# Output projection of the second layer as seven products of quarters per two token tiles, with the gate folded into weight forms made during the attention

## The chip, the cores and the metric

The kernel runs on one core of one Trainium2 chip. The core has a matrix engine (PE, TensorE), a vector engine (DVE, VectorE), an activation engine (ACT, ScalarE), a general engine (POOL, GpSimd) and a queue engine for transfers (SP, SyncE). They run side by side, each through its own instructions in order, and wait for one another by semaphores. The metric is the device time of one execution in microseconds, lower is better; the time before is the median of three runs.

## The reference, cut to what matters

Two layers work on 1024 latent tokens of width 1024, with 256 context tokens in front. The first layer mixes by windowed attention, the second by latent attention (16 heads, 64 wide). Only the end of the second layer is touched:

```python
ox = lax.map(lambda qq: attend(qq[0], qq[1], kn_all, kr_all, v_all), ...)   # softmax attention
ox = jnp.moveaxis(ox, 0, 1).reshape(b, T, B_WIDTH)
yx = (ox * jax.nn.silu(gx)) @ w_out          # (1024 x 1024) @ (1024 x 1024): the output projection
...
x = x + gate_x[:, None] * yx                 # gate_x: one factor per output column
...
return rms_norm(x, final_g)                  # x / sqrt(mean(x*x) + eps) * final_g, per token
```

All matrix products keep nearly full float precision: each operand is cut into a high part (rounded to the format that TensorE takes) and a low part (the rest), and a product is three matmuls, high x high, low x high, high x low (`mm3`, lines 283 to 287).

## The kernel before

The program builds one long list of instructions. From line 1081 on the order of the instructions on every engine is the order in which the program writes them. A planner (class Plan) reorders a stretch before the attention of the second layer and ends at line 1987; the units and the output stage that follow are not planned.

**The units.** The attention of the second layer runs in 16 units (class UnitB): 8 pairs of heads times two halves of 512 tokens. In the loop of line 2003 unit `ui` goes through ten steps c, one per 128 keys. A step holds, in written order: six score matmuls (`score`, line 1813) for the 512 queries of both heads; `top` of the next unit (line 1779, four or eight matmuls into two banks of PSUM), followed by two VectorE maxima over these banks (lines 1785 and 1787); in step 0, the gate multiplications of an earlier unit on GpSimd (`gate`, line 1858) and their store to `og_d` (line 1860); the other four score matmuls; and one exponential on ScalarE from PSUM (line 1823) into a ring of nine buffers, added by GpSimd into a running sum (lines 1827 and 1829; in the last unit by VectorE). The banks of `top` come from a ring of three (`topb`, banks 0, 1, 2), two per step. Scores use banks 3 to 6, in pairs, and bank 7 takes the product with the values (`PV`, line 1836). Behind the ten steps come PV, the sums by a column of ones (`fin2`, line 1847), the maxima turned into the next unit's shift (line 1797), two reciprocals (`inv`, line 1853), and for some units keys (`make_K`) or values (`make_V`) of later ones.

**The weights.** `wo_pieces` (line 1872) is a generator. Each call loads one piece of b_w_out (128 x 512) and splits an earlier one into `WoB`: a ScalarE copy makes the high part (line 280), a GpSimd subtraction the low part (line 281). It is called in step 2 of units 1 to 11, in step 7 of unit 6, and in steps 2 and 7 of units 12 and 13, 16 pieces in all.

**The output stage.** `out_tiles` (line 1916) goes over 8 tiles of 128 tokens. For each, `fetch_out` has loaded the gated attention (`og_d`) and x, `cut_out` has split it, and two halves of 512 columns take 8 x 3 matmuls each, over 8 chunks of 128 channels. From PSUM VectorE multiplies by the gate `gx1` (line 1948) and adds x (line 1949), ScalarE sums squares (line 1950), GpSimd makes the reciprocal root (lines 1960 to 1962), and VectorE scales by it and by final_g (line 1972) ahead of the store. The last 256 columns of the last tile use weights with the gate folded in (`fold_gate`, lines 1911 to 1914, GpSimd) and take x by two matmuls against an identity.

Transfers named `load` are issued by SP, in written order; one that has to wait holds up those behind it.

## Time and profile before

| | us |
|---|---|
| median of 3 runs | 1486.98 (1486.8 to 1489.12) |
| the profiled execution, its time | 1486.25 |
| its span in the profile | 1484.2 |
| TensorE busy | 1463.4 |
| VectorE busy | 1063.3 |
| ScalarE busy | 736.9 |
| GpSimd busy | 804.4 |

The granted TensorE clock was 0.999 of full speed. In the rows that follow, a row of the time line gives the start in us from the span's start, the busy time in us, the engine, the line of the kernel, the operation, what is written and read, how often (x4: four such instructions merged into one row), and in brackets how long the engine had been idle and what released it. A row of a line's view gives the count, the shortest, median and longest time in ns, the first and last start, and the shapes. PEld is the load of weights into TensorE, which overlaps its matmuls.

### The profile page before, as it was taken

To read this page: it belongs to the slowest core of one execution; us is meant where nothing else is said; L and a number is where in the kernel's file an instruction comes from. 1 tells how busy PE (TensorE), PEld (TensorE's weight loads), DVE (VectorE), ACT (ScalarE), POOL (GpSimd) and SP (SyncE) were. 2 spreads that over 40 slices of the span, in tenths; PEclk is the share of its full clock that TensorE was granted. 3 is DMA by queue.
4 is the path that set the end of the run, shared out by engine and by line. 5 is a ranking of instruction groups with operands and counts; after the bars stand their busy time and mean duration, and the time that the engine had idled before them with its cause. 6 is when DMAs were issued, how large, how long until landed. Compare 5 with 4: busy or idle time off the path is not lost.

```text
span 1484.2 us, 25103 instructions
## 1 busy us (share of the span) xinstructions
PE 1463.4 (99%) x9050; PEld 1184.9 (80%) x9050; DVE 1063.3 (72%) x2031; ACT 736.9 (50%) x1405; POOL 804.4 (54%) x736
## 2 busy tenths in 40 slices
PE   7999999999999999999999999999999999999998
PEld 4888888888888888889888888767777767866687
DVE  4787789738778888877988777666576566566764
ACT  4421222359888878877554432443454344444321
POOL 2463366356454444456300240798788788789371
PEclk9999999999999999999999999999999999999999
DMA  9555644573343333338344566011122211120442
GB/s 336 171 171 172 212 153 166 192 240 113 120 141 121 101 100 100 100 99 261 99 116 121 173 237 200 16 46 48 53 61 68 60 47 61 54 68 28 154 149 86
DMA packets 146964, 186.01 MB, mean 125 GB/s; under 512 B 12812, under 2 KB 100492, under 8 KB 146840
## 3 DMA queue, kind: packets, MB, share of 16 engines
q1 hardware_dynamic: 141864, 177.75, 38.0%
q10 hardware_dynamic: 4976, 6.66, 1.3%
q8 instruction: 71, 1.16, 0.3%
q14 instruction: 53, 0.43, 0.1%
HBM read 134.02 MB, written 46.15 MB: 121 GB/s over the span
## 4 chain that ended last, share of the span: by engine, by line
PE 91%; DVE 4%; issue 2%; DMA 1%; ACT 1%; POOL 1%; SPq 0%; ACTq 0%; POOLq 0%; DVEq 0%
PE PB L285 15%; PE PB L286 14%; PE PB L287 14%; PE PB L1813 13%; PE PB L1836 9%; PE PB L737 5%; PE PB L1779 5%; PE PB L727 5%; PE PB L697 3%; PE PB L698 3%; PE PB L911 1%; PE PB L1847 1%; DVE arena_r L281 1%; PE PB L916 1%; PE PB L756 1%
## 5 line engine op out<-in xcount | busy, mean ns | idle before, releaser
L285 PE MATMUL PB<-arena_r 128*128 128x512 f32 (+2 forms) x1200 | 439.4, 366 | 1.1 <-DVE arena_f L1261 1.1
L286 PE MATMUL PB<-arena_r 128*128 128x512 f32 (+2 forms) x1200 | 433.7, 361 | 0.1
L287 PE MATMUL PB<-arena_r 128*128 128x512 f32 (+2 forms) x1200 | 433.3, 361 | 0.0
L1829 POOL TENSOR_TENSOR arena_f<-arena_f 128x1024 f32<-128x1024 f32 x120 | 285.7, 2381 | 8.2
L285 PEld LDWEIGHTS PB<-arena_r 128*128 128x128 f32 x1200 | 226.3, 189 | 45.7 <-issue 9.0
L287 PEld LDWEIGHTS PB<-arena_r 128*128 128x128 f32 x1200 | 226.3, 189 | 33.4
L286 PEld LDWEIGHTS PB<-arena_r 128*128 128x128 f32 x1200 | 226.4, 189 | 32.1 <-POOL arena_r L281 0.6
L1813 PE MATMUL PB<-arena_r 64*128 64x512 f32 (+1 forms) x1600 | 225.9, 395 | 0.0
L1823 ACT ACTIVATE arena_f<-PB 128x1024 f32<-128x1024 f32 x160 | 164.3, 1027 | 112.1 <-PE PB L1813 83.8
L1785 DVE TENSOR_REDUCE krF<-PB 128x1 f32<-128x512 f32 (+1 forms) x264 | 166.9, 677 | 66.2 <-PE PB L1779 66.2
L1813 PEld LDWEIGHTS PB<-arena_r 64*128 64x128 f32 (+1 forms) x1600 | 173.7, 185 | 17.2 <-issue 5.2
L704 DVE CUSTOM_DVE_ANT_0 arena_f<-PB,arena_f,small 128x256 f32<-128x256 f32 (+1 forms) x288 | 148.2, 525 | 51.6 <-PE PB L698 33.3
L280 ACT CAST arena_r<-PB 128x512 fp32r<-128x512 f32 (+2 forms) x207 | 115.2, 563 | 113.9 <-PE PB L287 73.3
L281 DVE TENSOR_TENSOR arena_r<-PB,arena_r 128x512 fp32r<-128x512 f32 (+2 forms) x207 | 134.2, 660 | 36.4 <-ACT arena_r L280 36.0
L1836 PE MATMUL PB<-arena_f 128*64 128x512 f32 x640 | 145.9, 595 | 0.0
L281 POOL TENSOR_TENSOR arena_r<-arena_f,arena_r 128x512 fp32r<-128x512 f32 (+1 forms) x64 | 88.2, 1393 | 103.9 <-ACT arena_r L280 92.9
L280 ACT CAST arena_r<-arena_f 128x512 fp32r<-128x512 f32 (+1 forms) x142 | 82.2, 610 | 90.1 <-PE PB L287 29.5
L710 ACT ACTIVATE arena_f<-arena_f,small 128x640 f32<-128x640 f32 (+2 forms) x160 | 119.1, 744 | 15.5 <-DVE small L704 13.9
L507 DVE SCALAR_TENSOR_TENSOR arena_f<-arena_f,small 128x512 f32<-128x512 f32 x98 | 114.0, 1208 | 9.7 <-DMA arena_f<-ada_w 9.4
L737 PE MATMUL PB<-arena_r 128*128 128x512 f32 x336 | 118.6, 429 | 0.0
L1779 PE MATMUL PB<-arena_r 64*128 64x512 f32 (+1 forms) x768 | 110.6, 355 | 0.1
L727 PE MATMUL PB<-ident,arena_f 128*128 128x128 f32 x672 | 108.7, 272 | 0.1
(219 smaller groups left out, 2079.1 us busy)
## 6 DMA issues: line engine op xcount, KB each, us to landing
arena_f<-ada_w SPq DMA_DIRECT2D x96, 256.0 KB, 3.9
arena_r<-q_d SPq DMA_DIRECT2D x160, 128.0 KB, 2.8
arena_f<-a_w_in SPq DMA_DIRECT2D x40, 256.0 KB, 3.5
arena_f<-b_w_in SPq DMA_DIRECT2D x36, 256.0 KB, 3.2
arena_f<-x SPq DMA_DIRECT2D x16, 512.0 KB, 6.0
q_d<-arena_f SPq DMA_DIRECT2D x16, 512.0 KB, 3.0
arena_r<-qn_d SPq DMA_DIRECT2D x16, 512.0 KB, 5.1
g_d<-arena_f ACTq DMA_DIRECT2D x20, 256.0 KB, 3.9
```

The costliest lines, as they stand in the source:

```text
L280: nc.scalar.copy(hi, src)
L281: (lo_eng or nc.vector).tensor_sub(lo, src, hi.bitcast(F32))
L285: nc.tensor.matmul(o, ah, bh, start=first, stop=False)
L286: nc.tensor.matmul(o, al, bh, start=False, stop=False)
L287: nc.tensor.matmul(o, ah, bl, start=False, stop=last)
L727: nc.tensor.transpose(pt[:, h, :], self.Ps[h][:, ci * 128 : ci * 128 + 128], ident)
L737: nc.tensor.matmul(self.pv, V[:, self.chunks[ci], self.g, :], PT[:, s], start=ci == 0 and s == 0, stop=ci == self.m - 1 and s == 1,)
L1779: nc.tensor.matmul(bank[:, o : o + n], self.q[r, s, bs], k[r, 0, n0 : n0 + n], start=s == 0, stop=s == 2)
L1785: nc.vector.reduce_max(self.mxp[:, e, b : b + 1, i], bank[:, 0:n], AX.X)
L1813: nc.tensor.matmul(PB[:, b + e, :], k[r, s, cs], q[r, sq], start=i == 0, stop=i == 4)
L1829: eng.tensor_add(acc, acc, E)
L1836: nc.tensor.matmul(PB[r, 7, :], Vq[:, c, h, :], E[:, e], start=c == 0, stop=c == NT - 1)
```

## The change

Two tiles of 128 tokens (rows a1, a2, each in two halves of 512 channels: a11, a12, a21, a22) times the weight in four quarters of 512 x 512 (B11, B12, B21, B22) is made from seven products of 128 x 512 by 512 x 512 instead of eight. With the gate folded in (each column times its gate factor), the weight forms are B11, B21, B22, T1 = B12 - B11, T2 = B22 - T1, T3 = B22 - B12 and T4 = T2 - B21. The left sides are a11, a12, a22, s1 = a21 + a22, s2 = s1 - a11, s3 = a11 - a21 and s4 = a12 - s2. The order of the products is a11 B11, a12 B21, s2 T2, s3 T3, s1 T1, s4 B22, a22 T4, and sums of their results give the four quarters of the output. There are four such sets.

The weight forms are made by a new `wo_pieces`, one small piece of work per call, called in steps 1 to 6 of every unit from unit 2 on until it is used up: a multiplication by the gate, a difference, or a cut (ScalarE copy, then a VectorE subtraction). 18 of the 28 cuts go by one buffer, `wtmp`, to DRAM (`wb_d`) and are loaded back later (`wo_back`): ten for k = 2, 3 in units 13 and 14, T3 in the last unit and behind it, T4 in the first set of the output stage. The left sides are made by `all_cuts`, three of them behind the last steps of the last unit, two behind it, one more with each product. `out_sets` replaces `out_tiles`; the last unit's `fin2`, `inv` and `gate` move into its first set, behind the first, second and third product.

```diff
-    WoB = [r_at(o, 2, 1024) for o in (56, 64, 72, 96, 104, 48, 80, 88)]
+    homes = {
+        "B11": (56, 76, 80, 118), "B22": (60, 96, 84, 122), "T1": (64, 100, 88, 126), "T2": (68, 104, 92, 130),
+        "B21": (72, 108, 114, 134), "T3": (0, 4, 8, 12), "T4": (16, 20, 24, 28),
+    }
+    WB = {n: [r_at(o, 2, 512) for o in at] for n, at in homes.items()}
+    away = [(n, k) for n in homes for k in range(4) if k > 1 or n in ("T3", "T4")]
+    away = {at: wb_d[i] for i, at in enumerate(away)}
...
+    gx1 = r_at(48, 1024).bitcast(F32)
+    wtmp = r_at(52, 2, 512)
+    def wo_cut(n, k, src):
+        dst = wtmp if (n, k) in away else WB[n][k]
+        split(dst[:, 0], dst[:, 1], src)
+        if (n, k) in away:
+            load(out=away[n, k], in_=wtmp.bitcast(F32))
+    def wo_back(n, k):
+        load(out=WB[n][k].bitcast(F32), in_=away[n, k])
     def wo_pieces():
...
+        g1, g2 = gx1[:, 0:512], gx1[:, 512:1024]
+        def fetch(dst, i, j, k):
+            load(out=dst, in_=t["b_w_out"][i * 512 + k * 128 : i * 512 + k * 128 + 128, j * 512 : j * 512 + 512])
+        def fetch_abc(k, what):
+            for dst, i, j in what:
+                if k < 4:
+                    fetch(dst, i, j, k)
+        V = nc.vector
+        load(out=gx1, in_=gate_d[1, 0, :].partition_broadcast(128))
+        fetch_abc(0, ((a, 0, 0), (b, 0, 1), (c, 1, 1)))
+        yield
+        for k in range(4):
+            V.tensor_mul(a, a, g1)
+            yield
+            wo_cut("B11", k, a)
+            yield
+            V.tensor_mul(b, b, g2)
+            yield
+            V.tensor_sub(a, b, a)
+            yield
+            wo_cut("T1", k, a)
+            yield
+            V.tensor_mul(c, c, g2)
+            yield
+            wo_cut("B22", k, c)
+            yield
+            V.tensor_sub(b, c, b)
+            yield
+            wo_cut("T3", k, b)
+            fetch(b, 1, 0, k)
+            yield
+            V.tensor_sub(c, c, a)
+            yield
+            wo_cut("T2", k, c)
+            fetch_abc(k + 1, ((a, 0, 0),))
+            yield
+            V.tensor_mul(b, b, g1)
+            yield
+            wo_cut("B21", k, b)
+            yield
+            V.tensor_sub(b, c, b)
+            yield
+            wo_cut("T4", k, b)
+            fetch_abc(k + 1, ((b, 0, 1), (c, 1, 1)))
+            yield
...
+    rawr = [[r_at(o, 8, 128) for o in at] for at in ((138, 142), (48, 52))]
+    xr1 = Ring(F, [52, 56, 38, 48], 1024)
+    yr = Ring(F, [22, 26, 30, 34], 1024)
+    sr1 = Ring(F, [4, 6, 8, 44, 46], 512)
+    ur = Ring(F, [10, 12, 14, 16, 18, 20], 512)
+    cuts = [[r_at(o, 4, 128), r_at(l, 4, 128)] for o, l in ((146, 148), (112, 150), (32, 34), (36, 38), (40, 42), (44, 46))]
+    pso1 = Banks(0, 1, 2, 3, 4, 6)
+    WAY = ("B11", "B21", "T2", "T3", "T1", "B22", "T4")
+    cut_n = [0]
+    def cut(src, eng):
+        hi, lo = cuts[cut_n[0] % 6]
+        cut_n[0] += 1
+        split(hi, lo, src if len(src.shape) == 3 else shp(src, 4, 128), eng)
+        return hi, lo
+    def cut_set(n):
+        (a11, a12), (a21, a22) = ([x.bitcast(F32)[:, 4 * h : 4 * h + 4] for h in range(2)] for x in rawr[n % 2])
+        P = nc.gpsimd
+        eng = P if n == 0 else nc.vector
+        s1, s2, s3, s4 = (shp(sr1.next(), 4, 128) for _ in range(4))
+        yield cut(a11, eng)
+        yield cut(a12, eng)
+        P.tensor_add(s1, a21, a22)
+        P.tensor_sub(s2, s1, a11)
+        yield cut(s2, eng)
+        P.tensor_sub(s3, a11, a21)
+        yield cut(s3, nc.vector)
+        yield cut(s1, nc.vector)
+        P.tensor_sub(s4, a12, s2)
+        yield cut(s4, nc.vector)
+        yield cut(a22, P)
+    def all_cuts():
+        for n in range(4):
+            yield from cut_set(n)
+    def out_product(A, name, cs=slice(0, 512)):
+        ps = pso1()[:, cs]
+        for k in range(4):
+            mm3(ps, [A[s][:, k] for s in range(2)], [WB[name][k][:, s, cs] for s in range(2)], k == 0, k == 3)
+        return ps
...
+        for n in range(4):
+            xa, xb = xs
+            ya, yb = yr.next(), yr.next()
+            sa, sb = sm_ring(), sm_ring()
+            last = n == 3
+            for j in range(7):
+                if not (last and j == 6):
+                    ps = out_product(A.pop(0), WAY[j])
+                x = next(made, None)
+                if x:
+                    A.append(x)
+                while late:
+                    late.pop(0)()
+                if j == 0:
+                    p1 = ur.next()
+                    nc.scalar.copy(p1, ps)
+                    if n:
+                        tile_out(2 * n - 1, *prev)
+                if j == 1:
+                    V.tensor_add(ya[:, lo], ps, p1)
+                    quad(ya, xa, lo, sa, 0)
+                if j == 5 and n < 2:
+                    fetch_raw(n + 2)
+                if n == 0 and j == 0:
+                    u.fin2(psd)
+                if n == 0 and j in (1, 2):
+                    u.inv(j - 1)
+                    u.gate(256 * j - 256, 256 * j)
+                if n == 0 and j == 2:
+                    for k in range(4):
+                        wo_back("T4", k)
+                if j == 2:
+                    u2 = ur.next()
+                    V.tensor_add(u2, ps, p1)
+                if j == 3:
+                    u3 = ur.next()
+                    V.tensor_add(u3, ps, u2)
+                if j == 4:
+                    u4 = ur.next()
+                    V.tensor_add(u4, ps, u2)
+                    V.tensor_add(yb[:, up], ps, u3)
+                    quad(yb, xb, up, sb, 1)
+                    if n < 3:
+                        xs = fetch_x(n + 1)
+                if j == 5:
+                    V.tensor_add(ya[:, up], ps, u4)
+                    quad(ya, xa, up, sa, 1, lambda sa=sa: tile_rstd(sa))
+                    if last:
+                        P.tensor_add(u3, u3, xb[:, lo])
+                if j == 6 and not last:
+                    tile_out(2 * n, ya, sa)
+                    V.tensor_sub(yb[:, lo], u3, ps)
+                    quad(yb, xb, lo, sb, 0, lambda sb=sb: tile_rstd(sb))
+                    prev = yb, sb
+        W = A.pop(0)
+        r = sb[:, 3:4]
+        ts = slice(896, 1024)
+        halves = [slice(256 * h, 256 * h + 256) for h in range(2)]
+        for h, cs in enumerate(halves):
+            ps = out_product(W, "T4", cs)
+            if h == 0:
+                while late:
+                    late.pop(0)()
+                tile_out(6, ya, sa)
+            V.tensor_sub(yb[:, cs], u3[:, cs], ps)
+            square(yb, cs, sb, 2 if h else 0)
+            if h == 0:
+                V.tensor_add(sb[:, 0:1], sb[:, 0:1], sb[:, 1:2])
+                V.tensor_scalar(sb[:, 0:1], sb[:, 0:1], 1.0 / D, EPS, ALU.mult, ALU.add)
+                V.tensor_mul(yb[:, up], yb[:, up], fg[:, up])
+                V.tensor_mul(yb[:, cs], yb[:, cs], fg[:, cs])
+        V.scalar_tensor_tensor(sb[:, 2:3], sb[:, 2:3], 1.0 / D, sb[:, 0:1], ALU.mult, ALU.add)
+        P.tensor_tensor(r, sb[:, 2:3], mhalf, ALU.pow)
+        nc.scalar.activation(yb[:, up], yb[:, up], AF.Copy, scale=r)
+        V.scalar_tensor_tensor(yb[:, cs], yb[:, cs], r, fg[:, cs], ALU.mult, ALU.mult)
+        V.tensor_scalar_mul(yb[:, halves[0]], yb[:, halves[0]], r)
+        load2(out=out[ts, up], in_=yb[:, up])
+        load(out=out[ts, lo], in_=yb[:, lo])
...
-                first = fetch_out(0)
+                fetch_raw(0)
                 pu.inv(1)
                 pu.gate(256, 512)
-                got = fetch_out(1)
+                fetch_raw(1)
+                made = all_cuts()
+                A = []
             u.score(c, 0, CUT)
             if nu:
                 nu.top(PIECES[c])
             if c == 0 and ui > 1:
                 units[ui - 2].gate()
             u.score(c, CUT, 5)
-            if 0 < ui < 12 and c == 2 or ui == 6 and c == 7 or ui in (12, 13) and c in (2, 7):
+            if 1 < ui and 0 < c < 7:
                 next(wo_fill, None)
+            if ui in (13, 14) and c == 1:
+                for n, k in away:
+                    if k == ui - 11 and n not in ("T3", "T4"):
+                        wo_back(n, k)
             if nu is None and c == 0:
-                load(out=gx1, in_=gate_d[1, 0, :].partition_broadcast(128))
-                load(out=fg, in_=t["final_g"].partition_broadcast(128))
+                for k in range(2):
+                    wo_back("T3", k)
+            if nu is None and c > 6:
+                A.append(next(made))
         if nnu:
             nnu.prep()
         if nu is None:
...
             for _ in fill:
                 pass
         else:
-            ready = cut_out(first)
+            for k in range(2, 4):
+                wo_back("T3", k)
+            xs = fetch_x(0)
+            load(out=fg, in_=t["final_g"].partition_broadcast(128))
+            A += [next(made) for _ in range(2)]
         u.fin()
-    u.fin2(psd)
-    for j in range(2):
-        u.inv(j)
-        u.gate(256 * j, 256 * j + 256)
-    out_tiles(ready, got)
+    out_sets(A, made, xs, u)
     in_order.__exit__(None, None, None)
```

## The prediction

> **What bounds the kernel now.** I read the page's busy times and chain first, then the output stage, then the time line of one attention unit.

> ```profile
> span 1484.2 us, 25103 instructions
> PE 1463.4 (99%) x9050; PEld 1184.9 (80%) x9050; DVE 1063.3 (72%) x2031; ACT 736.9 (50%) x1405; POOL 804.4 (54%) x736
> PE 91%; DVE 4%; issue 2%; DMA 1%; ACT 1%; POOL 1%; SPq 0%; ACTq 0%; POOLq 0%; DVEq 0%
> L285 PE MATMUL PB<-arena_r x136: 277/389/500, 1390.0 to 1477.4; 128*128 128x512 f32 x120, 128*128 128x256 f32 x16
> 1450.67 0.39 PE L285 MATMUL PB<-arena_r 128*128 128x512 f32 x1
> 1451.35 0.39 PE L285 MATMUL PB<-arena_r 128*128 128x512 f32 x1
> 1390.00:1477.00 87.00, 87.00 (x406) 72.93 (x405) 51.85 (x66) 19.19 (x47) 40.20 (x60) 1.00 0.38 121
> 1341.00:1358.00 17.00, 17.00 (x152) 13.92 (x152) 13.13 (x21) 9.84 (x10) 16.53 (x9) 1.00 0.09 32
> ```

> TensorE is busy 99% of the span and 91% of the chain that ended last, so only work taken from it, or work that makes it wait, moves the end. In the output stage it never pauses: L285 opens each group of three matmuls, and 1451.35 - 1450.67 = 0.68 us per group is 0.227 us for one of 512 columns. L285 counts 120 + 16/2 = 128 full widths, three lines make 384, and 384 x 0.227 = 87 us. The two window rows (busy us of PE, weight load, DVE, ACT, POOL; then clock, DMA) are the output stage and ten scoring steps of unit 14. In the latter VectorE is busy 13.13 of 17 us and GpSimd 16.53.

> Those steps close up, in order of time:

> ```profile
> 1343.50 0.63 PE L1779 MATMUL PB<-arena_r 64*128 64x512 f32 x4
> 1343.66 1.29 POOL L1858 TENSOR_TENSOR arena_f<-arena_f,arena_r 128x512 f32<-128x512 f32 x1
> 1343.95 1.33 PE L1813 MATMUL PB<-arena_r 64*128 64x512 f32 x10
> 1344.15 1.29 DVE L1785 TENSOR_REDUCE krF<-PB 128x1 f32<-128x512 f32 x2 [0.32 <-PE PB L1779]
> 1344.68 1.03 ACT L1823 ACTIVATE arena_f<-PB 128x1024 f32<-128x1024 f32 x1 [0.56 <-PE PB L1813]
> 1345.11 0.62 PE L1779 MATMUL PB<-arena_r 64*128 64x512 f32 x4
> 1345.77 1.29 DVE L1785 TENSOR_REDUCE krF<-PB 128x1 f32<-128x512 f32 x2 [0.33 <-PE PB L1779]
> 1346.73 0.62 PE L1779 MATMUL PB<-arena_r 64*128 64x512 f32 x4
> 1348.77 19.58 POOL L1829 TENSOR_TENSOR arena_f<-arena_f 128x1024 f32<-128x1024 f32 x8
> ```

> A step lasts 1346.73 - 1345.11 = 1.62 us. In it VectorE makes two maxima from PSUM, 1.29 us, and has 0.33 us left. GpSimd adds the exponentials back to back, 19.58/8 = 2.45 us each. The maxima's banks are a ring of three and a step takes two, so the second matmul of the next L1779 group (1345.11 + 0.12) writes the bank that the first maximum of this step frees at 1344.15 + 0.65 = 1344.80. VectorE may therefore be about 0.42 us late; what comes on top, TensorE waits for.

> **The change, part by part.** *Weights made in the units.* There were 16 splits of b_w_out, ACT copy and GpSimd subtraction. Now wo_pieces yields 61 times, one per step for c = 1 to 6 from unit 2, so through unit 11 and one step of unit 12; the first issues only loads, and 60 steps each carry one VectorE instruction of 128x512 with two SBUF inputs: 32 products or differences and 28 low parts of cuts (each behind an ACT copy). Queues run in written order here, so each stands on VectorE between the maxima of step c and those of c+1; behind it wait these maxima, and for them TensorE's next L1779 group, with the scores behind that.

> Its price alone is 0.65 us (1.29/2 below). By VectorE's work alone six steps overrun by 6 x (1.29 + 0.65 - 1.62) = 1.9, less 0.42 slack 1.5 a unit, **15 us** in ten units: the lower bound. A cut costs more: its copy stands behind the step's exponential (ends 1344.68 + 1.03 = 1345.71), takes 0.61, and the subtraction ends at 1346.97, the maximum behind it at 1347.62 in place of 1346.42, and the L1779 group that needs its bank at 1346.85 is 0.8 late. 28 x 0.8 + 32 x 0.32 - 10 x 0.42 = **28 us**, still with every instruction at its lone price. But the lone price does not hold beside GpSimd. From the first layer, and from the output stage:

> ```profile
> 199.75 0.68 DVE L281 TENSOR_TENSOR arena_f<-arena_f 128x512 fp32r<-128x512 f32 x1
> 199.93 1.64 POOL L597 TENSOR_TENSOR arena_f<-arena_f 128x512 f32<-128x512 f32 x1 [0.55 <-DVE arena_f L596]
> 200.34 3.48 DVE L507 SCALAR_TENSOR_TENSOR arena_f<-arena_f,small 128x512 f32<-128x512 f32 x2
> 201.65 1.62 POOL L599 TENSOR_TENSOR arena_f<-arena_f 128x512 f32<-128x512 f32 x1
> L507 DVE SCALAR_TENSOR_TENSOR arena_f<-arena_f,small x98: 730/752/1849, 71.6 to 296.2; 128x512 f32<-128x512 f32 x98
> 1080.26 0.61 ACT L280 CAST arena_r<-arena_f 128x512 fp32r<-128x512 f32 x1
> 1449.53 1.29 DVE L281 TENSOR_TENSOR arena_r<-arena_r 128x512 fp32r<-128x512 f32 x2
> L1829 POOL TENSOR_TENSOR arena_f<-arena_f x120: 2352/2377/2417, 931.8 to 1366.0; 128x1024 f32<-128x1024 f32 x120
> ```

> L507 takes 0.75 us in the median and 3.48/2 = 1.74 here; the POOL instructions beside it take 1.64 and 1.62 instead of 1.29. The ends interleave: POOL to 201.57, then VectorE to about 202.1, POOL to 203.27, VectorE to 203.82. They take turns, one whole instruction each. The 120 adds of the attention vary only from 2352 to 2417 ns, since no VectorE instruction with two SBUF inputs stands beside them before unit 15. The change puts 60 there. A fill that arrives during an add waits for its end, the next add waits for the fill, and the step becomes one add and one fill: 2.45 + 0.65 = 3.1 us. Longer it does not stay, as there is one add per step and GpSimd would go idle. So (3.1 - 1.62) x 60 = 89, less 10 x 0.42, **84 us**. Above that lie only the two gate multiplications of each unit (1.29 + 0.07 each), 27 us if all fall in these steps: upper bound 111. I take 84: the pair of rows above has the same two engines and forms as the fill, and GpSimd is 97% busy where it falls.

> [...]

> The 18 stores and 18 reloads of 512 KB are hidden: DMA's share there is 0.09. One buffer (wtmp) serves all stores, so a copy waits for the store before it; a store of that size lands in 2.7 us (below) and cuts are two steps apart, 3.2 us or more. Without this cover it is some 0.3 us per stored cut. The 16 GpSimd subtractions removed return 16 x 1.29 us to an engine that TensorE did not wait for.

> *The output stage.*

> ```profile
> x_d<-arena_f SPq DMA_DIRECT2D x10, 512.0 KB, 2.7
> arena_r<-og_d SPq DMA_DIRECT2D x8, 512.0 KB, 4.5
> 1380.19 5.66 ACT L1823 ACTIVATE arena_f<-PB 128x1024 f32<-128x1024 f32 x5 [5.01 <-PE PB L1813]
> 1384.71 4.51 PE L1836 MATMUL PB<-arena_f 128*64 128x512 f32 x20
> 1386.24 1.14 ACT L280 CAST arena_r<-arena_r 128x512 fp32r<-128x512 f32 x2 [0.39 <-DMA arena_r<-og_d]
> 1394.26 0.99 POOL L1858 TENSOR_TENSOR arena_f<-arena_f 128x256 f32<-128x256 f32 x1 [0.18 <-DVE arena_f L1853]
> 1448.20 1.42 DVE L1972 SCALAR_TENSOR_TENSOR arena_f<-arena_f,small 128x512 f32<-128x512 f32 x2 [2.03 <-POOL small L1962]
> 1458.49 0.55 POOL L1962 TENSOR_TENSOR small<-small 128x1 f32<-128x1 f32 x1
> 1463.71 0.63 ACT L1950 ACTIVATE arena_f<-arena_f 128x512 bf16<-128x512 f32 x1 [4.81 <-DVE arena_f L1949]
> 1466.51 0.69 DVE L1948 TENSOR_TENSOR arena_f<-PB,arena_r 128x512 f32<-128x512 f32 x1 [2.90 <-PE PB L287]
> 1477.62 0.28 PE L287 MATMUL PB<-arena_r 128*128 128x256 f32 x1
> 1478.00 0.38 ACT L1946 ACTIVATE arena_f<-PB 128x256 bf16<-128x256 f32 x1 [1.69 <-PE PB L287]
> ```

> (a) Matmuls: four sets of 7 x 12 = 336 for 384, **-10.9 us**. (b) Start: the first cut's ACT copy now stands before the exponential of step 8, and its data came at 1386.2, when all five exponentials had ended (1385.85). Two of them now follow it, and the last PV step ends about **1 us** later (0 to 2). (c) T4 returns from DRAM for the seventh product, due 6 x 2.72 + 1.0 = 17.3 us after the attention's last matmul (1389.2). Its four loads stand on SP behind the last gate's store. That gate ended at 1395.25, 6 us after it; now it comes one product later (2.7) and behind GpSimd's cuts and one add (some 2), so 11; four loads of 512 KB, the first 4.5 us, all by about 9: 20, so **3 us** (0 to 9). (d) Per set, VectorE has six low parts (0.65) and four final scalings (0.71), GpSimd nine 512-column instructions (1.36): 6.7 + 12.2 = 18.9 us that must take turns, in 84 x 0.227 = 19.1 us. I take 1 us per set, **4 us** (0 to 12). (e) Tail: tile 6 needs the product before the last, and its two scalings stand on VectorE ahead of the last quarter. From that product's end: VectorE 0.9, two GpSimd adds to 3.6, reciprocal root (0.93 and hand-offs) to 4.7, scalings to 6.2, difference 6.6, square 7.3, small ones 7.7, gains 8.8, second difference 9.2, and only then the last square; TensorE is done at 2.9. Before, the square began 0.1 us after TensorE (1477.90, 1478.00): **+6 us** (3 to 8). Sum (a) to (e): -10.9 + 1 + 3 + 4 + 6 = **+3** (-8 to +18 or so).

> Total: 84 + 3 = +87. The profiled execution took 1486.25 us (span 1484.2 and 2.05 around it); the median of the runs is 0.73 above it. 1486.25 + 87 = **1573 us**. All low ends together give 1493, all high ends 1615.

> **The rivals.** *Fills at their lone price:* GpSimd is often between adds when a fill comes, and the wait is rare. For it: a slower TensorE gives GpSimd time to catch up. Against: 19.58 us without a gap. 28 + 3 - 4 (less turn-taking in (d)) = +27, **1513**. *Faster:* VectorE's free time absorbs the fills. For it: 17 - 13.13 = 3.9 us free per ten steps is just 6 x 0.65. Then the stage alone counts, -10.9 + 1 + 2 = -8, **1478**. Against: that time is 0.33 us in each step, and three banks let only 0.42 be carried over; it decides from a fill of 0.33 us. [...] *The saving is not there:* fewer matmuls, but no shorter stage; this is in my sum, (b) to (e).

> **How the numbers follow.** Forecast (taking turns, 1540 to 1605) 0.66; lone price (1500 to 1540) 0.17; half clock 0.05; both gates and a fuller output stage above 1605, 0.06; faster 0.05; no change 0.01. A measurement of this kernel can tell 0.2%, 3 us, from no change. Slower 0.94, same 0.01, faster 0.05. The range 1503 to 1605 leaves out the first, the half clock and the extreme, and part of the lone price; the likeliest case alone is 1540 to 1605.

> **What would show it.** Right: units 2 to 11 some 8 us longer each, units 12 to 14 as before; in them VectorE waiting in its 128x512 instructions (1.5 us or more mean), the adds of L1829 at about 3.0 where a fill stands, and TensorE's L1779 released by VectorE. In the output stage 336 matmuls with a stall before the first set's seventh product and 12 us or more from TensorE's end to the span's. Wrong: fills at 0.65 us with the adds at 2.38 (lone price), units of 26 us (hidden), or a granted clock below 1.00.

## The result, and the profile after

The changed kernel took 1579.84 us (median of 6 runs, 1578.25 to 1584.44); the kernel before, run beside it, 1486.99 us (6 runs). The ratio is 1.0627, 95% interval 1.0613 to 1.0642: 6.3% slower. The profiled execution took 1581.25 us.

The page of the changed kernel: its span, its busy times, and the chain that ended last, by engine.

```profile
span 1579.1 us, 25144 instructions
PE 1481.2 (94%) x8988; PEld 1172.1 (74%) x8988; DVE 1150.6 (73%) x2093; ACT 751.7 (48%) x1433; POOL 820.6 (52%) x724
PE 73%; DVE 15%; POOL 4%; issue 3%; DMA 2%; ACT 2%; SPq 0%; POOLq 0%; DVEq 0%; ACTq 0%
```

TensorE's share of the chain fell from 91% to 73%; VectorE's rose from 4% to 15%. 94.9 us were added to the span. Where they lie follows from a few moments of the time line: the first unit's maxima are turned at 925.0 us (924.0 before), the last unit's at 1441.3 (1362.8), the last matmul of PV ends at 1469.28 (1389.22), TensorE's last matmul at 1565.4 (1477.9), the span at 1579.1 (1484.2). So the units grew by 77.5 us, the last unit's end by 1.6, the output stage by 14.9 (95.0 to 109.9), and 0.9 was there before the units. In the views below and in the rest of the text a fill is one of the 60 VectorE instructions that make the weight forms, and half clock is a granted TensorE clock of 0.50, as in the window 992.13 to 995.54 of the changed kernel.

**The units.** Windows of the changed kernel (us, busy of PE, weight load, DVE, ACT, POOL, then clock and DMA): ten scoring steps of unit 14, without fills; 12 us of steps with fills in unit 4; the output stage's matmuls but for the last 0.2 us; and the rest of the span.

```profile
1420.00:1437.00 17.00, 17.00 (x152) 14.16 (x150) 13.13 (x21) 9.48 (x10) 14.87 (x8) 1.00 0.51 187
1067.00:1079.00 12.00, 8.55 (x70) 6.02 (x66) 11.70 (x13) 5.84 (x8) 11.61 (x6) 1.00 0.26 87
1469.30:1565.20 95.90, 84.90 (x352) 66.94 (x352) 47.25 (x63) 26.24 (x58) 57.14 (x58) 0.93 0.44 151
1565.20:1579.10 13.90, 0.18 (x2) 0.00 (x0) 4.23 (x11) 3.18 (x9) 4.36 (x7) 0.64 0.20 75
```

Without fills TensorE is busy in all 17.00 us of the ten steps, as before. With them VectorE counts as busy 11.70 of 12 us and GpSimd 11.61, and TensorE only 8.55. The time line of such steps, changed kernel, selected rows:

```profile
1065.23 2.46 POOL L1834 TENSOR_TENSOR arena_f<-arena_f 128x1024 f32<-128x1024 f32 x1 [10.00 <-ACT arena_f L1830]
1067.30 0.94 DVE L282 TENSOR_TENSOR arena_r<-arena_f,arena_r 128x512 fp32r<-128x512 f32 x1 [0.68 <-ACT arena_r L281]
1067.77 13.85 POOL L1836 TENSOR_TENSOR arena_f<-arena_f 128x1024 f32<-128x1024 f32 x5
...
1074.93 1.67 DVE L1899 TENSOR_TENSOR arena_f<-arena_f,arena_r 128x512 f32<-128x512 f32 x1
1076.52 1.27 DVE L1792 TENSOR_REDUCE krF<-PB 128x1 f32<-128x512 f32 x2
1077.25 0.72 PE L1786 MATMUL PB<-arena_r 64*128 64x512 f32 x3 [0.89 <-DVE krF L1792]
1077.72 1.67 DVE L282 TENSOR_TENSOR arena_r<-arena_f,arena_r 128x512 fp32r<-128x512 f32 x1
```

From one fill to the next it is 1077.72 - 1074.93 = 2.79 us, where a step took 1.62. GpSimd's five additions take 13.85/5 = 2.77 each: the same period. A fill lasts 1.67 in place of 0.65, because it waits for the addition under way. The first shows the turn exactly: the addition of 1065.23 ends at 1067.69, the fill, which began at 1067.30, ends at 1068.24, 0.55 later. It is so for all of them: 54 of the 60 fills in this trace met a GpSimd instruction, and each ended 0.55 or 0.56 us after that instruction's end; the other six took 0.68. The next addition loses only about 0.35 of that (2.71 us, where one with no fill beside it takes 2.37), as the start of one overlaps the end of the other. Then the maxima follow, and TensorE's L1786 waits 0.89 us for them.

The intervals between the starts of one unit's exponentials (L1823 before, L1830 after) tell two sorts of unit apart:

```
before, unit 6:  1.59 1.61 1.62 1.64 1.64 1.65 1.64 1.65
after,  unit 5:  1.61 1.62 1.63 2.81 2.78 2.79 2.78 2.79   unit +5.8 us
after,  unit 6:  1.58 1.63 4.34 2.81 3.26 2.78 3.26 2.79   unit +9.4 us
after,  unit 7:  1.59 1.62 5.06 2.48 3.56 2.78 3.27 2.79   unit +10.1 us
```

Six units, unit 5 among them, are 5.8 or 5.9 us longer: five steps of 2.8, the first fill being free, since it comes ahead of GpSimd's first addition. Units 6, 7 and 11 grew by 9.4 to 10.1: there the first fill is a cut, which stands behind its copy and so meets the first addition. Unit 2 grew by 9.7; there the first multiplication waited 3.08 us for the load of its operand, issued only one step ahead. Unit 12, with a single cut, which is its first fill, grew by 4.2. That makes the 77.5.

**The output stage.** From the attention's last matmul to TensorE's last it is 96.1 us with 336 matmuls, in place of 88.7 with 384. Rows of the changed kernel, in order of time but for the last: TensorE's stalls at 1490.56, 1531.08 and 1556.93, and what the other engines do in one set.

```profile
1490.56 0.77 PE L286 MATMUL PB<-arena_r 128*128 128x512 f32 x1 [3.45 <-DMA arena_r<-wb_d]
1505.68 0.56 ACT L2033 COPY arena_f<-PB 128x512 f32<-128x512 f32 x1
1517.57 1.29 POOL L2010 TENSOR_TENSOR arena_f<-arena_f 128x512 f32<-128x512 f32 x1 [2.65 <-DVE arena_f L2058]
1518.82 1.29 POOL L1972 TENSOR_TENSOR arena_f<-arena_r 128x512 f32<-128x512 f32 x1
1520.14 0.62 ACT L281 CAST arena_r<-arena_f 128x512 fp32r<-128x512 f32 x1 [4.57 <-POOL arena_f L1972]
1520.79 0.69 DVE L282 TENSOR_TENSOR arena_r<-arena_f,arena_r 128x512 fp32r<-128x512 f32 x1 [3.30 <-ACT arena_r L281]
1521.40 0.69 DVE L2063 TENSOR_TENSOR arena_f<-PB,arena_f 128x512 f32<-128x512 f32 x1
1522.17 1.66 POOL L2010 TENSOR_TENSOR arena_f<-arena_f 128x512 f32<-128x512 f32 x1 [2.06 <-DVE arena_f L2063]
1531.08 0.52 PE L286 MATMUL PB<-arena_r 128*128 128x512 f32 x1 [3.10 <-ACT arena_r L281]
1531.56 0.56 ACT L2033 COPY arena_f<-PB 128x512 f32<-128x512 f32 x1
1556.93 0.80 PE L286 MATMUL PB<-arena_r 128*128 128x512 f32 x1 [4.01 <-ACT arena_r L281]
1505.68:1531.56 25.88, 22.78 (x100) 18.33 (x98) 12.02 (x18) 7.09 (x18) 14.54 (x15) 1.00 0.38 123
```

The first copy of a set (L2033) comes 25.88 us after that of the set before, and a set is 84 matmuls of 0.227 = 19.1. In these 25.88 us (last row, a window) VectorE is busy 12.02, GpSimd 14.54 and ScalarE 7.09: none of the three is full. They wait for each other in a ring. GpSimd adds x (L2010) when VectorE has its sum (L2058), then makes the next left side (L1972), ScalarE copies it, VectorE makes its low part (L282), and only then its next sum (L2063), for which GpSimd waits again. Four such additions make a set; here they start at 1510.10, 1517.57, 1522.17 and 1527.89. TensorE runs ahead of this ring (the window holds 100 of its matmuls, not 84) and lives on left sides made ahead until they run out.

### The profile page after: what moved, and what is told of

The parts are those of the page before. It is cut to its first block, busy times and chain, and to the rows that moved or that the text cites. A ratio compares the mean times of both kernels' runs of the same rounds, so it can differ in the third digit from the quotient of the medians.

```text
span 1579.1 us, 25144 instructions
## 1 busy us (share of the span) xinstructions
PE 1481.2 (94%) x8988; PEld 1172.1 (74%) x8988; DVE 1150.6 (73%) x2093; ACT 751.7 (48%) x1433; POOL 820.6 (52%) x724
## 3 DMA queue, kind: packets, MB, share of 16 engines
q8 instruction: 71, 1.16, 0.3%
## 4 chain that ended last, share of the span: by engine, by line
PE 73%; DVE 15%; POOL 4%; issue 3%; DMA 2%; ACT 2%; SPq 0%; POOLq 0%; DVEq 0%; ACTq 0%
PE PB L286 12%; PE PB L287 12%; PE PB L288 12%; PE PB L1843 8%; PE PB L1820 7%; PE PB L738 5%; PE PB L728 5%; DVE arena_r L282 4%; DVE krF L1792 4%; PE PB L1786 3%; PE PB L698 2%; PE PB L699 2%; POOL arena_f L2010 1%; PE PB L912 1%; DVE krF L1794 1%
## 5 line engine op out<-in xcount | busy, mean ns | idle before, releaser
L286 PE MATMUL PB<-arena_r 128*128 128x512 f32 (+2 forms) x1180 | 435.5, 369 | 11.6 <-ACT arena_r L281 7.1
L287 PE MATMUL PB<-arena_r 128*128 128x512 f32 (+2 forms) x1180 | 429.7, 364 | 0.5 <-DVE arena_r L282 0.4
L288 PE MATMUL PB<-arena_r 128*128 128x512 f32 (+2 forms) x1180 | 428.2, 363 | 0.0
L1836 POOL TENSOR_TENSOR arena_f<-arena_f 128x1024 f32<-128x1024 f32 x120 | 297.2, 2477 | 25.8 <-ACT arena_f L1830 18.3
L286 PEld LDWEIGHTS PB<-arena_r 128*128 128x128 f32 x1180 | 223.7, 190 | 59.4 <-ACT arena_r L281 13.3
L1830 ACT ACTIVATE arena_f<-PB 128x1024 f32<-128x1024 f32 x160 | 164.1, 1026 | 179.7 <-PE PB L1820 153.5
L288 PEld LDWEIGHTS PB<-arena_r 128*128 128x128 f32 x1180 | 223.9, 190 | 33.6
L287 PEld LDWEIGHTS PB<-arena_r 128*128 128x128 f32 x1180 | 224.0, 190 | 33.3 <-DVE arena_r L282 1.5
L1820 PE MATMUL PB<-arena_r 64*128 64x512 f32 (+1 forms) x1600 | 239.5, 399 | 0.0
L1820 PEld LDWEIGHTS PB<-arena_r 64*128 64x128 f32 (+1 forms) x1600 | 181.6, 188 | 22.3 <-issue 5.2
L1786 PE MATMUL PB<-arena_r 64*128 64x512 f32 (+1 forms) x768 | 137.5, 375 | 57.2 <-DVE krF L1792 48.4
L281 ACT CAST arena_r<-PB 128x512 fp32r<-128x512 f32 (+2 forms) x207 | 115.2, 563 | 113.6 <-PE PB L288 73.5
L281 ACT CAST arena_r<-arena_f 128x512 fp32r<-128x512 f32 (+1 forms) x170 | 99.4, 611 | 141.9 <-PE PB L288 29.4
L282 DVE TENSOR_TENSOR arena_r<-PB,arena_r 128x512 fp32r<-128x512 f32 (+2 forms) x207 | 134.3, 661 | 36.8 <-ACT arena_r L281 36.4
L1786 PEld LDWEIGHTS PB<-arena_r 64*128 64x128 f32 x768 | 87.8, 188 | 84.8 <-DVE krF L1792 67.6
L282 DVE TENSOR_TENSOR arena_r<-arena_f,arena_r 128x512 fp32r<-128x512 f32 (+1 forms) x121 | 113.5, 959 | 41.5 <-ACT arena_r L281 41.3
L711 ACT ACTIVATE arena_f<-arena_f,small 128x640 f32<-128x640 f32 (+2 forms) x160 | 119.0, 744 | 15.5 <-DVE small L705 13.9
L282 POOL TENSOR_TENSOR arena_r<-arena_f,arena_r 128x512 fp32r<-128x512 f32 (+1 forms) x49 | 68.9, 1424 | 105.3 <-ACT arena_r L281 94.5
## 6 DMA issues: line engine op xcount, KB each, us to landing
arena_f<-x_d SPq DMA_DIRECT2D x18, 512.0 KB, 5.1
wb_d<-arena_r SPq DMA_DIRECT2D x18, 512.0 KB, 2.9
arena_r<-wb_d SPq DMA_DIRECT2D x18, 512.0 KB, 6.0
arena_f<-x SPq DMA_DIRECT2D x16, 512.0 KB, 5.6
```

Source lines behind the costliest of these rows:

```text
L281: nc.scalar.copy(hi, src)
L282: (lo_eng or nc.vector).tensor_sub(lo, src, hi.bitcast(F32))
L286: nc.tensor.matmul(o, ah, bh, start=first, stop=False)
L287: nc.tensor.matmul(o, al, bh, start=False, stop=False)
L288: nc.tensor.matmul(o, ah, bl, start=False, stop=last)
L1786: nc.tensor.matmul(bank[:, o : o + n], self.q[r, s, bs], k[r, 0, n0 : n0 + n], start=s == 0, stop=s == 2)
```

## The experiments

Each is one execution with its profile; the kernel before took 1486.3 to 1486.8 us beside them. The six times of the changed kernel differ by up to 6.2 us, so terms of a few us are read from the traces. "Stage" is the time from the attention's last matmul to the end of the span.

**1. No weight forms.**

```diff
-        for k in range(4):
-            V.tensor_mul(a, a, g1)
-            yield
-            wo_cut("B11", k, a)
...
+        split(wtmp[:, 0], wtmp[:, 1], a, nc.gpsimd)
+        for at in away.values():
+            load(out=at, in_=wtmp.bitcast(F32))
+            yield
...
```

> The weight forms are not computed: one cut is made and copied to all places by transfers only, so the output projection has the right sizes and the wrong numbers; the 60 VectorE instructions and all but one of the 28 ScalarE copies are gone from the units, the output stage is unchanged. If the fills alone lengthen the attention, the units return to 26.3 to 33.8 us as before the change, the last PV matmul of the attention ends about 1390, and the time is 1487 + 15 = 1502 us (the changed output stage took 109.8 us from there to the end against 95.1). Rival: the reloads and stores of the forms, or the new output stage's early cuts, cost the attention part of the 78 us; then the units stay above 30 us and the time above 1520.

1506.65 us. The units are as before but for the one that holds the one cut (+3.7); the stage is 110.0. The whole cost in the units comes from the fills with their ScalarE copies, none from the stores and loads of the forms, and the stage alone loses 15.

**2. No running sums on GpSimd.**

```diff
-                eng.tensor_add(acc, self.E[0], E)
-            elif c:
+                eng.tensor_add(acc, self.E[0], ones[:, 0:1].unsqueeze(2).to_broadcast([128, 2, 512]))
+            elif c and self.i == NU - 1:
```

> In units 0 to 14 GpSimd's running sum of the exponentials is left out from step 2 on (a sum of the first exponential and ones stands in its place, so the softmax is wrong); fills stay in steps 1 to 6. If the fills take turns with the adds for whole instructions, a fill takes about 0.68 us without them and the attention is some 28 us longer than before the change (the lone price), the time about 1487 + 28 + 15 = 1530. Rival: the fills are slow by themselves, or TensorE waits on ScalarE's copies and not on VectorE: the fills stay near 1.66 us or the time near 1575.

1535.4 us; the last PV ends 34.6 us later than in the kernel before (80.1 in the changed one). One line's view of this kernel:

```profile
L1913 DVE TENSOR_TENSOR arena_f<-arena_f x4: 680/680/684, 1023.5 to 1262.1; 128x512 f32<-128x512 f32 x4
```

The same line took 1.66 in the changed kernel. Of the 60 fills 48 are at their lone price here; the other 12 meet what GpSimd still does in the units. They cost 34.6 all the same; the other 45 come from GpSimd's additions beside them.

**3. Additions of half the length.**

```diff
-            if c == 1:
-                eng.tensor_add(acc, self.E[0], E)
-            elif c:
-                eng.tensor_add(acc, acc, E)
+            if c:
+                first = self.E[0] if c == 1 else acc
+                for e in range(2) if self.i < NU - 1 else (slice(0, 2),):
+                    eng.tensor_add(acc[:, e], first[:, e], E[:, e])
```

> Each of GpSimd's adds of 1024 columns in units 0 to 14 is written as two of 512; the sums are the same. If VectorE waits for the end of the whole GpSimd instruction that runs when it comes, its wait is halved: fills of 1.1 to 1.3 us in place of 1.66, steps of about 2.4 in place of 2.78 us, and the time about 20 us shorter, 1560. Rival: the two engines share a port at a fixed rate, element by element: a fill stays at about 1.66 us, the steps at 2.8 and the time at 1575 to 1585.

1573.13 us, neither the theory's number nor, by 2 us, the rival's. The time line of this kernel:

```profile
1074.65 8.37 POOL L1836 TENSOR_TENSOR arena_f<-arena_f 128x512 f32<-128x512 f32 x6
1076.36 1.80 DVE L282 TENSOR_TENSOR arena_r<-arena_f,arena_r 128x512 fp32r<-128x512 f32 x1
1078.09 2.57 DVE L1792 TENSOR_REDUCE krF<-PB 128x1 f32<-128x512 f32 x4
```

A fill still takes 1.80 us, although an addition is now 1.29 (the median of its line). VectorE comes back after two maxima, 1.27 us; by then the first half has ended, the second has begun, and the fill waits for that one. So the wait is for one whole instruction, and which one is a matter of phase. Two other accounts fall. With a wait of fixed length all fills that meet an addition would last alike; those of L282 last from 0.93 to 1.81 us here. With the rival's sharing, element by element, the end of a fill would not hang on the end of an addition; all 53 fills that met one here ended 0.55 to 0.64 us after its end.

**4. Fills moved out of the scoring steps.**

```diff
-            if 1 < ui and 0 < c < 7:
-                next(wo_fill, None)
...
+            for _ in range(3 if ui > 1 else 0):
+                next(wo_fill, None)
             nu.shift()
...
             for _ in fill:
-                pass
+                if ui > 1:
+                    next(wo_fill, None)
```

> The same 60 fills are called three per unit between the next unit's turn and its shift (where VectorE idles 4.6 us waiting for TensorE), and one with each piece of keys or values that a unit makes, and none in the scoring steps. If the 78 us come from the place among the maxima, the steps return to 1.62 us and the time to 1502 to 1515 us, with some units a few us longer where three fills and their waits exceed 4.6 us. Rival: the turns with GpSimd cost TensorE wherever they lie (the adds come late and the ring of exponentials fills up): the time stays above 1540.

1548.83 us, the last PV 47.6 later than before. The scoring steps are back at 1.62 but for the first of some units; the fills now hold up VectorE where the next unit's queries and keys are made. The time line of this kernel:

```profile
1005.45 2.01 DVE L1899 TENSOR_TENSOR arena_f<-arena_f,arena_r 128x512 f32<-128x512 f32 x1 [7.63 <-DMA arena_f<-b_w_out]
1014.73 0.79 PE L1786 MATMUL PB<-arena_r 64*128 64x512 f32 x1 [3.60 <-DVE arena_r L282]
```

The expected 1502 to 1515 was wrong: here too TensorE soon stands behind VectorE's queue. The time is in the rival's range, but the steps of 1.62 speak against the rival's reason. Part of it is no price of a fill: the first row waited 7.63 us for the load of its operand, another fill 2.30.

**5 and 6. Half of the fills.** In one, the 28 cuts are left out; in the other, the 32 products and differences.

```diff
     def wo_cut(n, k, src):
         dst = wtmp if (n, k) in away else WB[n][k]
-        split(dst[:, 0], dst[:, 1], src)
         if (n, k) in away:
             load(out=away[n, k], in_=wtmp.bitcast(F32))
+        else:
+            load(out=dst.bitcast(F32), in_=away["T3", 0])
...
+        split(wtmp[:, 0], wtmp[:, 1], a, nc.gpsimd)
+        load(out=away["T3", 0], in_=wtmp.bitcast(F32))
```

> The changed kernel with the 32 products and differences of the weight forms as they are and the 28 cuts left out (no ScalarE copy, no low part; their transfers stay, the stored bytes are not the forms, so the output is not the reference's). The units grew by 78 us in the changed kernel. Theory (a fill's step is one add and one fill, 2.78 us for 1.62, and the rest of the 78 comes from cuts that wait for ScalarE's copy, after which TensorE's clock is halved for some 3 us): 32 x 1.16 = 37 us, less up to 32 x 0.42 us of slack that the empty steps between renew, so 24 to 37 us, all units at a clock of 1.00, time about 1527 to 1540. Rival (every fill costs the same, 78/60 = 1.3 us): 42 us, 1544 or more.

```diff
         for k in range(4):
-            V.tensor_mul(a, a, g1)
             yield
             wo_cut("B11", k, a)
...
```

> The changed kernel with the 28 cuts as they are and the 32 products and differences left out (the cuts are of the raw weights, so the output is not the reference's). Theory: a cut costs the step of 2.78 us and, where its copy is late, a pause of TensorE of 2.3 us or more with half clock behind it: 28 x 1.16 = 32 us and 8 to 14 us of half clock, so 38 to 48 us, units with a clock below 1.00 among them, time about 1541 to 1552. Rival (every fill costs the same, 1.3 us): 36 us, 1540 or less, clock 1.00 in all units.

1555.71 and 1579.16 us; the last PV 54.6 and 78.0 us later than before. No price that was expected held: run 5's time is in its rival's open range (1544 or more), but not at the 42 us that the rival names, and run 6 is far above both of its own. Its half clock came as the theory had it, in stretches of 3.4 or 6.8 us in nine of the eleven units with fills (granted 0.87 to 0.96 in windows of 24 and 38 us). 28 cuts alone cost what all 60 fills cost together. Groups of VectorE from 975 to 1340 us (busy, mean ns | idle before them), first of the kernel without cuts, then of the one with cuts only, then of the changed kernel:

```profile
L1916 DVE TENSOR_TENSOR arena_f<-arena_f 128x512 f32<-128x512 f32 x4 | 11.2, 2788 | 0.0
L1906 DVE TENSOR_TENSOR arena_f<-arena_f,arena_r 128x512 f32<-128x512 f32 x4 | 4.8, 1192 | 0.0
```

```profile
L282 DVE TENSOR_TENSOR arena_r<-arena_f,arena_r 128x512 fp32r<-128x512 f32 x27 | 50.0, 1852 | 28.0 <-ACT arena_r L281 28.0
```

```profile
L282 DVE TENSOR_TENSOR arena_r<-arena_f,arena_r 128x512 fp32r<-128x512 f32 x27 | 47.7, 1767 | 5.4 <-ACT arena_r L281 5.4
```

A fill with an empty step beside it meets an addition at any point, or none: the means by line range from 1.19 to 2.79 us, where most fills in steps one after another settle into one phase and wait 1.0. Cuts alone lose more: steps between them are short again, so VectorE also waits 28.0 us for ScalarE's copies, 5.4 with all fills. So the cost of the fills is not a sum over fills. Without cuts, unit 2 grew by 9.3, part of it a wait of 5.1 us for a GpSimd cut that I put there; the other 29 products and differences cost 43.5, 1.5 each, the 28 cuts 2.7 each (76.4 in the units), all 60 together 1.3. How much of the cuts' price is phase, how much copies and how much clock was not separated.

**7 to 9. Three orders of queues in the output stage.** First s4 sooner:

```diff
         P.tensor_sub(s2, s1, a11)
+        P.tensor_sub(s4, a12, s2)
         yield cut(s2, eng)
...
-        P.tensor_sub(s4, a12, s2)
         yield cut(s4, nc.vector)
```

> The changed kernel with one GpSimd subtraction moved: s4 = a12 - s2 is made right behind s2, two cuts sooner, so that it no longer stands on GpSimd behind the addition of x to the set before. Theory (the stalls before the sixth products are an order of queues): the 3.1 and 4.0 us stalls of TensorE before the sixth product of the third and fourth set shrink below 1.5 us together, the half clock behind each goes, and the time falls by 8 to 12 us, to 1568 to 1572. Rival (VectorE and GpSimd, taking turns, are simply full: 18.9 of 19.1 us a set): the stalls stay as large and move to another product, time within 3 us of 1580.

1580.97 us, stage 107.9: a set takes 25.1 us in place of 25.9. The stalls before the sixth products did shrink, to 0.43 and 0.91 us; but others of 1.63 and 1.03 came, the mean granted clock was 0.989 as in the changed kernel, and the tail grew from 13.8 to 15.6. It is the rival's number, though, as run 11 shows, not for the rival's reason. Then T4 sooner:

```diff
             for k in range(2, 4):
                 wo_back("T3", k)
+            for k in range(3):
+                wo_back("T4", k)
...
-                    for k in range(4):
-                        wo_back("T4", k)
+                    wo_back("T4", 3)
```

> The changed kernel with three of the four loads of T4 issued behind those of T3, ahead of the output stage; the fourth, whose space is still used by the last gate, stays. Theory (TensorE waits for the last of four loads that stand behind the gate's store): the 3.45 us wait before the first set's seventh product falls to 0 to 1.5 us, its half clock goes, and the time falls by 4 to 6 us. Rival (the wait is set by the gate's end, not by the count of loads): the wait stays at 3 us or more, time within 2 us.

1581.33 us, stage 111.1. The time line of this kernel:

```profile
1490.60 0.50 PE L286 MATMUL PB<-arena_r 128*128 128x512 f32 x1 [2.67 <-DMA arena_r<-wb_d]
```

The wait fell from 3.45 to 2.67 and the half clock behind it was gone (1.00 in the window 1487 to 1493), yet nothing was gained: what TensorE saves here it waits later for the ring of the other three (4.04 and 3.50 us before later products). The wait is neither the theory's (0 to 1.5) nor the rival's (3 or more); the time is the rival's. Last, the tail:

```diff
...
-                tile_out(6, ya, sa)
             V.tensor_sub(yb[:, cs], u3[:, cs], ps)
...
+        tile_out(6, ya, sa, (0,))
         V.scalar_tensor_tensor(sb[:, 2:3], sb[:, 2:3], 1.0 / D, sb[:, 0:1], ALU.mult, ALU.add)
+        tile_out(6, ya, sa, (1,))
```

> The changed kernel with the two scalings of tile 6 moved behind the last difference, one on each side of the small instruction that ends the last sum of squares. Theory (the 13.9 us from TensorE's end to the span's end are VectorE's order: the last difference stands behind tile 6's root and scalings): they fall by 3 to 5 us to 9 to 11 us, and the time by as much. Rival (the chain through the last root and the stores sets the end anyway): less than 1 us.

1575.3 us; TensorE's end to the span's end is 12.3 in place of 13.8, a fall of 1.5 where 3 to 5 was expected; 1.9 of the difference in time is the stage's, the rest lies ahead of it.

**10. All three, no weight forms.** The edits of 1 and 7 to 9 together.

> The three moves of order together (s4 sooner, three loads of T4 sooner, tile 6 behind the last difference), and the weight forms not computed at all (space of theirs is filled by transfers and one cut), so the output is not the reference's: it shows what the output stage could be worth if the forms cost nothing. The same without the three moves took 1506.65 us with 110.0 us from the attention's last matmul to the end. Theory (the stage's losses are three orders of queues): 110.0 falls to 90 to 94 us and the time to 1487 to 1491, about the kernel before. Rival (turn-taking of VectorE and GpSimd bounds the stage): 100 us or more, 1496 or more.

1504.12 us, stage 106.6: the rival's number. Three orders were worth 3.4 us together, and a set still takes 25 us.

**11. x added by VectorE.**

```diff
         def quad(y, x, cs, st, c, more=lambda: None):
-            P.tensor_add(y[:, cs], y[:, cs], x[:, cs])
+            V.tensor_add(y[:, cs], y[:, cs], x[:, cs])
...
                     if last:
-                        P.tensor_add(u3, u3, xb[:, lo])
+                        V.tensor_add(u3, u3, xb[:, lo])
```

> The changed kernel with one edit: x is added to the four quarters of a set by VectorE in place of GpSimd, so that GpSimd no longer waits for VectorE's sums and the next left sides no longer stand behind that. Theory (one set lasts 25.9 us because VectorE's sum, GpSimd's addition, GpSimd's next left side, ScalarE's copy and VectorE's low part follow one another once per product, each engine idle half the time): the period of a set falls to 19 to 22 us, TensorE's stalls before the sixth products go, and the time falls by 8 to 15 us, to 1565 to 1572. Rival (turn-taking of VectorE and GpSimd fills the set, so work can only be shifted between them): the period stays at 25 us or more, time 1577 or more.

1564.78 us, at the low end of what the theory had. The first copies of three sets in this kernel, and the window of one set:

```profile
1499.45 0.57 ACT L2033 COPY arena_f<-PB 128x512 f32<-128x512 f32 x1
1520.40 0.57 ACT L2033 COPY arena_f<-PB 128x512 f32<-128x512 f32 x1
1541.33 0.57 ACT L2033 COPY arena_f<-PB 128x512 f32<-128x512 f32 x1
1499.45:1520.40 20.95, 20.95 (x94) 17.37 (x93) 17.96 (x21) 7.09 (x18) 9.41 (x11) 1.00 0.47 152
```

A set takes 20.95 us and TensorE has no pause in it; the stage is 95.9 in place of 109.9. One edit that gives VectorE more to do (17.96 in 20.95 us, 12.02 in 25.88 before) takes back 13.9 of the 14.9 us. It cuts the ring where GpSimd waited for VectorE's sums. The half clock behind two of the changed kernel's stalls goes with them (granted 0.98 from 1467.03 to 1553.00, where the changed kernel had 0.93 from 1469.30 to 1565.20); how much of the 13.9 is that was not separated.

**12. All four, no weight forms.** The edits of 10 and 11 together.

> The same edit with the three moves of order (s4 sooner, three loads of T4 sooner, tile 6 behind the last difference), and the weight forms not computed (their space filled by transfers and one cut), so the output is not the reference's. The three moves without this edit took 1504.12 us, 106.6 us of it from the attention's last matmul to the end, against 95.0 in the kernel before. Theory: 88 to 94 us and a time of 1486 to 1491, so that the stage's seven products are worth at most some 7 us even if their weights cost nothing. Rival: 102 us or more, 1500 or more.

1487.99 us against 1486.84 beside it, the stage 93.0 against 95.0. So even with the stage mended, and its weights for nothing, the seven products end where the eight did. No version that beats the kernel before was found.

## Why the prediction was right

The forecast was 1573 us by 84 in the units and 3 in the output stage; measured are 77.5 and 14.9, 1.6 at the last unit's end (forecast with the stage, as (b)), and 0.9 ahead of all. The sign and the main mechanism held; two sizes were off, and one reason was wrong. That the total is only 7 us off is partly luck: the units came out 6.5 us lower, and the stage with (b) 13.5 higher.

| step | predicted | measured | from |
|---|---|---|---|
| fills in the units | 84 (15 to 111) | 77.5 | turns of the maxima, after less before |
| (a) matmuls | -10.9 | -10.9 | 336 for 384 x 0.227 |
| (b) start | +1 | +1.6 | last unit's end |
| (c) T4 and (d) turns | +3, +4 | +18.3 together | 96.1 - 88.7 + 10.9 |
| (e) tail | +6 | +7.5 | 13.8 - 6.3 |

*Fills.* That VectorE and GpSimd take turns by whole instructions, beside 2.4 us additions too, is shown by the rows above, by run 2 (no additions: 48 fills at 0.68) and by run 3. The mis-sized term is "one add and one fill: 2.45 + 0.65 = 3.1 us": the step is 2.79, since about 0.3 us of each hand-over overlaps. It was also taken for all 60 fills; an ordinary unit grew by 5.8, not by some 8. The first of a unit is mostly free, while a cut that meets the unit's first addition costs a step of 4.3 or more, and unit 2's load was late. These nearly cancel: by ordinary units alone it would be 58 (ten times 5.8); the three units with such cuts and unit 2 add 15, unit 12 adds 4. A step of 1.29 + 1.0 + 0.65 = 2.94 and a sum of 75, an estimate for a wait that ends after 1.0 us as in the prediction's rows of L507, would come near both numbers, but for a wrong reason: in the changed kernel most waits are 1.0 by phase, and others there and in run 5 go up to about 2.2.

*Lone price.* That lower estimate of 28 us had its test in run 2: 34.6, with 12 of the 60 fills not at the lone price and the late load of unit 2 in it.

*(c)* The wait was 3.45 us for 3, at the place that was named. Shortening it brought nothing all the same: in run 8 it was 2.67, with no half clock behind it, and the time stayed.

*(d)* is the step that failed. It added up busy times, 18.9 us that must take turns in 19.1, and so found a nearly full set with 1 us to lose. Measured, the two are busy 12.02 and 14.54 of 25.88 us. What counts is the ring of hand-overs in written order, once around for each of a set's four additions of x, and 13.9 us hang on one link of it, half clock included (run 11). I had costed each instruction of this stage and no chain through the queues.

*(e)* The chain of the tail is the one that was told, and its rows in the changed kernel are these:

```profile
1570.55 0.41 DVE L2082 TENSOR_TENSOR arena_f<-arena_f,PB 128x256 f32<-128x256 f32 x1
1572.80 0.41 DVE L2082 TENSOR_TENSOR arena_f<-arena_f,PB 128x256 f32<-128x256 f32 x1
1573.31 0.42 ACT L2007 ACTIVATE arena_f<-arena_f 128x256 bf16<-128x256 f32 x1 [1.74 <-DVE arena_f L2082]
```

The last difference ends at 1573.21, 7.8 us after TensorE, and the last square starts only then. Run 9 took back 1.5 of it.

*The rivals.* Half clock, which had a chance of 0.05, came, but not in every step with a fill: the clock was 1.00 in the lock step of 2.8 us (window 1067 to 1079) and, up to the end of the matmuls, fell only behind pauses of 2.29 to 4.01 us. In the units it cost little (unit 12, with it, grew by 4.2 in all; its ten score matmuls took 2.71 us instead of some 1.4), in the stage at most some 6 us by 0.07 of 84.9 busy us, an estimate. That the saving is not there was in the sum, and it is the fuller truth about the stage: run 12 finds 2 us of the 10.9.

## What to carry to other kernels

An engine's free time in a loop is worth only what one step can carry over: 0.33 us per step, 23% of VectorE's time, did not hide 60 instructions of 0.68 us; even without GpSimd's additions beside them they cost 34.6 us (run 2). Where four engines hand one item around, cost the ring in queue order, not their busy times: here VectorE, GpSimd and ScalarE were busy 46, 56 and 27% of 25.9 us per set, and moving GpSimd's additions of x to VectorE made it 20.95. And a price that depends on phase cannot be summed by instruction: 28 cuts cost as much as those 28 and 32 more.

## What the runs showed of the hardware

Two pauses of nearly the same length, in the changed kernel, and TensorE's clock behind each. Time line and windows, the last three of them intervals of a raster that is explained below:

```profile
1136.74 0.73 PE L1786 MATMUL PB<-arena_r 64*128 64x512 f32 x3 [2.25 <-DVE krF L1792]
1367.22 0.92 PE L1786 MATMUL PB<-arena_r 64*128 64x512 f32 x3 [2.30 <-DVE krF L1792]
1367.56 2.71 PE L1820 MATMUL PB<-arena_r 64*128 64x512 f32 x10
1136.70:1140.00 3.30, 2.38 (x22) 1.76 (x24) 3.30 (x5) 1.53 (x2) 2.43 (x2) 1.00 0.73 243
1367.20:1370.50 3.30, 3.28 (x19) 2.77 (x21) 1.84 (x3) 1.02 (x1) 1.82 (x2) 0.56 0.42 164
1132.08:1135.49 3.41, 2.41 (x21) 1.75 (x17) 2.61 (x3) 2.53 (x3) 2.33 (x1) 1.00 0.03 10
1135.49:1138.90 3.41, 1.90 (x14) 1.28 (x14) 3.41 (x5) 0.88 (x1) 2.75 (x2) 1.00 0.58 192
1364.18:1367.59 3.41, 1.11 (x11) 0.63 (x9) 3.41 (x3) 1.00 (x1) 3.33 (x2) 1.00 0.06 25
```
